# Differential heads' probabilities and two heads' rows turned by VectorE and transfers, in a decoder layer on one Trainium2 core

## The chip, the cores and the metric

One core of one Trainium2 chip runs the whole layer in one launch. The metric is the device time in microseconds, the median of three runs. All times below are microseconds unless marked ns.

The engines are called as in the profile: PE is TensorE, ACT is ScalarE, DVE is VectorE, POOL is GpSimd (used here to issue transfers), SP is SyncE (which issues the weight loads).

## The reference

A decoder layer in float32: half a SwiGLU feed-forward, a token mixer with two attention branches, another half feed-forward, with layer norms between. One batch, 256 positions, 2048 channels, 5632 hidden. The change lies in the mixer:

```python
def _diff_attention(q, k, v, positions, lam):
    ...
        s = jnp.einsum('bqhmd,bkhmd->bhmqk', q[:, q0:q1], k[:, :q1]).astype(jnp.float32) * scale
        dist = jnp.abs(pos[:, q0:q1, None] - pos[:, None, :q1])
        s = s - slopes[None, :, None, None, None] * dist[:, None, None, :, :]
        s = jnp.where(_causal_mask(q0, q1), s, -jnp.inf)
        p = jax.nn.softmax(s, axis=-1)
        a = (p[:, :, 0] - lam * p[:, :, 1]).astype(v.dtype)
        outs.append(jnp.einsum('bhqk,bkhd->bqhd', a, v[:, :q1]))

def _mixer(...):
    ...
    o_mla = _mla_attention(q, k, v_mla).reshape(b, s, MLA_V_COLS)
    o_diff = _diff_attention(...)
    o_diff = (_rms_norm(o_diff, subln_g) * (1.0 - lambda_init)).reshape(b, s, DIFF_V_COLS)
    y = jax.nn.sigmoid(gate_mla) * (o_mla @ w_br_mla) + jax.nn.sigmoid(gate_diff) * (o_diff @ w_br_diff)
    return y @ w_out
```

There are 4 differential heads, each with two maps of 128 channels and values of 256, and 8 MLA heads with values of 128.

## The kernel before

**Matmuls.** The 256 rows lie in two blocks (b = 0, 1) of 128. A large product is made in three matmuls (`triple`, L208 to L210) from a high and a low part of each operand, so that it keeps float32's precision. SP streams the weights into `raw` tiles of 512 KB (two k-tiles of 128x512). ACT casts each to its high part (`wring`, L154), DVE subtracts it from the raw tile for the low part (`wring`, L155), into a ring of 6 pairs in the mixer. One raw tile serves one **unit**, 12 matmuls (2 k-tiles x 3 x 2 blocks). A cast waits until PE has used the ring's pair.

**Order.** The program is written as a chain of units. `later(n, fn)` has `fn` issued n units further on; this is how the small work (softmax, turns, copies) is put between the units. The numbers in the `later` calls are thus a table of due times, and a scheduler sets the final order on each engine from what the program issues. Each engine then runs its own list in order.

**Mixer.** In order of units: a latent projection; the gates (rows kept in DRAM by `keep_gate`, L1197 and L1199); dq, dk (`pair_cols`, L1210) and dv; wuq, wuk and wuv for MLA; the last gate chunks; `branch_diff` for four quads f of 512 output channels (x = od, the differential heads' outputs); `branch_mla` for the same four (x = om). After that w_out takes y. The work of the differential heads (`diff_head`) is spread over the wuq, wuk and wuv units and the gates'.

**A differential head** has four steps: `scores` (8 matmuls, L1250, and two softmaxes; the difference p at L1259), `turn`, `values` (three pairs of matmuls, L1270 to L1272, then an RMS norm, `junk` on ACT and `orow` on DVE), `turn2` (orow turned and cast into `od`). p is 128 x 384: the block pairs (0,0), (1,0), (1,1).

**Turning.** What enters a matmul must have its channels, or keys, on the partitions. There are two ways to turn a 128x128 piece. One is a transpose on PE with the identity into a PSUM bank, followed by a copy (`p_cols` L1108, `turn2` L1290, `rows_to_quad` L671). The other is `turn` (L722): DVE transposes in blocks of 32x32 (`blocks`, L715), four transfers on POOL's queue write the rows to DRAM so that the blocks land in order (`turn`, L717), and `wait` units later one transfer reads it back (`turned`, L729); `more` units later it is used. Its channels lie in an order of their own, and the rows of the weight are put into the same order on the host (`_turned_rows`). `turn_p` (L1116) does this for the p of the MLA heads with one transfer out (`pturn`) and four back (`pt`).

**The gates back.** `get_gates(f)` (L1350) has POOL load the four gate tiles of quad f (two branches, two blocks, 256 KB each, L1354). `branch_mla(f)` makes the sigmoids on ACT (L1371), multiplies the diff branch by its gate (L1374), and when a block's product is done, L1375 and L1376 add the MLA branch. y of f = 0 and 1 is turned by transfers, y of f = 2 and 3 by PE (`rows_to_quad`, L671).

**POOL's queue** issues its transfers in list order, over 8 semaphores in turn: the ninth transfer after one waits for it to have landed.

Of the kernel before, what the change touches and what calls it, by code (L numbers as in the profile page):

```python
# [11 lines left out]
F32 = mybir.dt.float32  # L12
# [47 lines left out]
def layer_kernel(ctx: ExitStack, tc: tile.TileContext, a: dict, out: bass.AP):  # L60
# [27 lines left out]
    def tr_bank(name="tr"):  # L88
        return psum.tile([P, 512], F32, tag="tr", name=nm(name), bufs=3)
# [633 lines left out]
    def turn(row, use, wait, more):  # L723
        to = dram.tile([P, 512], F32, name=nm("turn"))
        turn_out(row, to)

        def back():
            t = tmp_tile([P, 512], "turned")
            nc.gpsimd.dma_start(t, to)  # L729
            later(more, lambda: use(turned(t)))  # L730
        later(wait, back)

    def turn_to_quad(row, b, x, q, wait, more):
        turn(row, lambda t: x.put(q, b, t), wait, more)

    def turn_to_cols(row, dst, b, wait, more):
        turn(row, lambda t: S.copy(dst[:, :, b * P:(b + 1) * P].rearrange("p k (i c) -> p k i c", i=4), t), wait, more)
# [367 lines left out]

    SEG = ((0, P), (P, 384))

    def p_cols(p):  # L1108
        t = tr_bank()
        for i in range(3):  # L1110
            PE.transpose(t[:, i * P:(i + 1) * P], p[:, i * P:(i + 1) * P], ident)
        pt = small.tile([P, 384], F32, tag="p", name=nm("pt"), bufs=3)
        S.copy(pt, t[:, 0:384])
        return pt

    def turn_p(p, keep, more):  # L1116

        t = tmp_tile([P, 384], "pblocks")
# [12 lines left out]
    def mixer(x):  # L1131
# [76 lines left out]
        def pair_cols(w, name):  # L1208
            dst = [act_tile([P, 4, T], F32, name) for _ in range(2)]

            def done(n, b, bank, snap, op):
                t = tmp_tile([P, 512], name + "r")
                whole(t, bank, snap, op)
                later(1, lambda: turn_to_cols(t, dst[n], b, 4, 10))
            hy.group(w[0], w[1], done, False, True)
            return dst

# [19 lines left out]
            project((a["wgm"], a["wgd"])[i][f], x, KD, 512, lambda b, bank: keep_gate(i, f, b, bank))  # L1237

        od = Acts(MH, "od")

        def diff_head(h):
            st = {}
# [18 lines left out]
                st["p"] = p1  # L1261

            def turn():
                st["pt"] = p_cols(st["p"])

            def values():
                pt = st["pt"]
                o = tr_bank()
                dvh = [t[:, h * DV:(h + 1) * DV] for t in dv]
                PE.matmul(o[:, 0:DV], pt[:, 0:P], dvh[0], start=True, stop=True)  # L1270
                PE.matmul(o[:, DV:2 * DV], pt[:, P:T], dvh[0], start=True, stop=False)
                PE.matmul(o[:, DV:2 * DV], pt[:, T:384], dvh[1], start=False, stop=True)  # L1272
                ss = sm(2, "oss")
                junk = tmp_tile([P, 512], "junk")
                for b in range(2):
                    S.activation(junk[:, b * DV:(b + 1) * DV], o[:, b * DV:(b + 1) * DV], AF.Square,
                                 accum_out=ss[:, b:b + 1])
                ms = sm(2, "oms")
                V.tensor_scalar(out=ms, in0=ss, scalar1=1.0 / DV, scalar2=None, op0=ALU.mult)
                r = rstd(ms, RMS_EPS, 2)  # L1280
                orow = tmp_tile([P, 512], "orow")
                for b in range(2):
                    V.scalar_tensor_tensor(out=orow[:, b * DV:(b + 1) * DV], in0=o[:, b * DV:(b + 1) * DV],
                                           scalar=r[:, b:b + 1], in1=subg, op0=ALU.mult, op1=ALU.mult)
                st["o"] = orow

            def turn2():
                t = tr_bank()
                for i in range(4):
                    PE.transpose(t[:, i * P:(i + 1) * P], st["o"][:, i * P:(i + 1) * P], ident)  # L1290
                tv = t.rearrange("p (b i t) -> p b i t", b=2, i=2)
                for b in range(2):
                    od.put(h // 2, b, tv[:, b], (h % 2) * 2, 2)
            return scores, turn, values, turn2

        for h in range(DH):
            for i, f in enumerate(diff_head(h)):
                later(2 + 5 * h + 3 * i + i // 3, f)
        qT = [cols_proj(a["wuq"][c], cn, 4, "qT") for c in range(2)]
        qrT = act_tile([P, 4, T], F32, "qrT")  # L1300

# [65 lines left out]
        def branch_mla(f):  # L1367
            g0, g1 = gates.pop(f)
            y = diff_rows.pop(f)
            for t in (g0, g1):  # L1370
                S.activation(t, t, AF.Sigmoid)  # L1371

            def done(b, bank):
                V.tensor_tensor(out=y[:, b, :], in0=y[:, b, :], in1=g1[:, b, :], op=ALU.mult)  # L1374
                V.tensor_tensor(out=g0[:, b, :], in0=bank, in1=g0[:, b, :], op=ALU.mult)  # L1375
                V.tensor_tensor(out=y[:, b, :], in0=y[:, b, :], in1=g0[:, b, :], op=ALU.add)  # L1376
                if f < 2:
                    later(1, lambda: turn_to_quad(y[:, b, :], b, yq, f, 4, 6))
                else:
                    later(2, lambda: rows_to_quad(y[:, b, :], b, yq, f))  # L1380
            project(a["wbm"][f], om, MH, 512, done)
# [74 lines left out]
def _layout(i):  # L1456
# [25 lines left out]
    r["wuk"] = _chunks(_turned_rows(_turned_cols(w["mla_w_uk"])), 512)  # L1482
    r["wuv"] = _chunks(_turned_rows(w["mla_w_uv"]), 512)
    r["wbm"] = _chunks(w["w_branch_mla"], 512)
    r["wbd"] = _chunks(w["w_branch_diff"], 512)
    r["w_out"] = _chunks(np.concatenate([_turned_rows(w["w_out"][:1024]), w["w_out"][1024:]]), 512)
    pos = i["positions"]
    r["pos_row"] = pos.reshape(1, T)
# [31 lines left out]
```

## Time and profile before

| | us |
|---|---|
| median of three runs | 1967.29 (1966.77 to 1968.22) |
| the profiled execution | 1969.03 |
| its span on the chip | 1967.3 |
| PE busy in it | 1951.7 (99%) |
| DVE busy | 1777.8 (90%) |
| ACT busy | 1249.7 (64%) |
| POOL busy | 309.3 (16%) |
| granted TensorE clock | 0.998 |

The span is the time from the first to the last instruction; the rest of the execution's time lies around it. A row of the timeline gives start, duration, engine, line, operation, out<-in, tile and how many of the same kind; in brackets, how long the engine was idle before, and what ended it. Matmuls overlap, so a row's duration is longer than its distance to the next. The stage of the differential heads runs from about 987 to 1074, the MLA heads from 1075 to 1143, `branch_mla` from 1143 to 1188.

### The profile page before, as it was taken

To read this page: it belongs to the slowest core of one execution; us is meant where nothing else is said; L and a number is where in the kernel's file an instruction comes from. 1 tells how busy PE (TensorE), PEld (TensorE's weight loads), DVE (VectorE), ACT (ScalarE), POOL (GpSimd) and SP (SyncE) were. 2 spreads that over 40 slices of the span, in tenths; PEclk is the share of its full clock that TensorE was granted. 3 is DMA by queue.
4 is the path that set the end of the run, shared out by engine and by line. 5 is a ranking of instruction groups with operands and counts; after the bars stand their busy time and mean duration, and the time that the engine had idled before them with its cause. 6 is when DMAs were issued, how large, how long until landed. Compare 5 with 4: busy or idle time off the path is not lost.

```text
span 1967.3 us, 25772 instructions
## 1 busy us (share of the span) xinstructions
PE 1951.7 (99%) x8760; PEld 1618.2 (82%) x8760; DVE 1777.8 (90%) x2183; ACT 1249.7 (64%) x1634; POOL 309.3 (16%) x531
## 2 busy tenths in 40 slices
PE   9999999999999999999999999999999999999997
PEld 8888888888888898888888887888888888888886
DVE  7999999998998879988987676789999999999986
ACT  6666766676655666666667654556676666765661
POOL 0112111122100010102241530001211112210000
PEclk9999999999999999999999999999999999999999
DMA  8978888878776666767685788678888878787773
GB/s 315 285 227 262 268 261 247 259 234 306 271 238 214 208 223 248 246 223 262 203 248 196 236 295 274 198 261 255 255 267 264 250 238 271 251 314 236 277 233 121
DMA packets 149779, 488.83 MB, mean 248 GB/s; under 512 B 21600, under 2 KB 21648, under 8 KB 149648
## 3 DMA queue, kind: packets, MB, share of 16 engines
q1 hardware_dynamic: 119088, 401.13, 59.5%
q0 software_dynamic: 30560, 86.07, 16.8%
q8 instruction: 68, 1.11, 0.2%
q14 instruction: 63, 0.52, 0.1%
HBM read 456.71 MB, written 30.41 MB: 248 GB/s over the span
## 4 chain that ended last, share of the span: by engine, by line
PE 92%; DMA 3%; DVE 1%; issue 1%; ACT 1%; POOL 1%; SPq 0%; DVEq 0%; POOLq 0%; ACTq 0%
PE mm L209 29%; PE mm L208 29%; PE mm L210 29%; DMA turned<-turn 1%; DMA gate<-gates 1%; PE tr L210 1%; PE tr L209 1%; PE tr L208 1%; DMA turn<-blocks 0%; POOL turn L717 0%; PE tr L671 0%; ACT wring L154 0%; DMA raw<-in_wgd_dram 0%; DMA raw<-in_gu_dram 0%; PE tr L1322 0%
## 5 line engine op out<-in xcount | busy, mean ns | idle before, releaser
L154 ACT CAST wring<-raw 128x1024 fp32r<-128x1024 f32 (+2 forms) x467 | 481.9, 1037 | 322.3 <-PE mm L210 236.7
L155 DVE TENSOR_TENSOR wring<-raw,wring 128x1024 fp32r<-128x1024 f32 (+2 forms) x467 | 557.4, 1201 | 91.7 <-ACT wring L154 89.4
L154 ACT CAST wring<-sraw 128x1024 fp32r<-128x1024 f32 x436 | 453.0, 1052 | 201.9 <-DVE sraw L428 85.7
L155 DVE TENSOR_TENSOR wring<-sraw,wring 128x1024 fp32r<-128x1024 f32 x436 | 520.7, 1219 | 23.6 <-ACT wring L154 20.7
L208 PE MATMUL mm<-wring,h 128*128 128x512 f32 (+2 forms) x1248 | 480.9, 385 | 0.0
L210 PE MATMUL mm<-wring,h 128*128 128x512 f32 (+2 forms) x1248 | 480.3, 385 | 0.0
L209 PE MATMUL mm<-wring,h 128*128 128x512 f32 (+2 forms) x1248 | 480.0, 385 | 0.0
L208 PE MATMUL mm<-wring,xs 128*128 128x512 f32 x776 | 302.2, 389 | 0.6 <-ACT snap L385 0.6
L209 PE MATMUL mm<-wring,xs 128*128 128x512 f32 x776 | 301.9, 389 | 0.0
L210 PE MATMUL mm<-wring,xs 128*128 128x512 f32 x776 | 301.9, 389 | 0.0
L208 PEld LDWEIGHTS mm<-wring,h 128*128 128x128 f32 x1248 | 234.5, 188 | 46.9 <-ACT h L154 0.6
L209 PEld LDWEIGHTS mm<-wring,h 128*128 128x128 f32 x1248 | 234.5, 188 | 46.5 <-DVE wring L155 0.4
L210 PEld LDWEIGHTS mm<-wring,h 128*128 128x128 f32 x1248 | 234.4, 188 | 46.5 <-DVE h L155 0.7
L428 DVE TENSOR_TENSOR sraw<-sraw,sraw 128x1024 f32<-128x1024 f32 x168 | 199.2, 1219 | 2.0 <-DMA sraw<-in_wgm_dram 1.2
L208 PEld LDWEIGHTS mm<-wring,xs 128*128 128x128 f32 x776 | 145.7, 188 | 31.2 <-ACT snap L385 1.0
L210 PEld LDWEIGHTS mm<-wring,xs 128*128 128x128 f32 x776 | 145.7, 188 | 30.2
L209 PEld LDWEIGHTS mm<-wring,xs 128*128 128x128 f32 x776 | 145.7, 188 | 30.1
L717 POOL DMA_DIRECT2D hT<-blocks x176 | 96.8, 562 | 367.0 <-DVE blocks L715 366.0
L209 PE MATMUL mm<-wring,x 128*128 128x512 f32 x336 | 130.8, 389 | 0.5 <-DVE wring L155 0.5
L208 PE MATMUL mm<-wring,x 128*128 128x512 f32 x336 | 130.8, 390 | 0.0
L210 PE MATMUL mm<-wring,x 128*128 128x512 f32 x336 | 130.6, 389 | 0.0
L430 POOL DMA_DIRECT2D sraw<-in_gu_dram x40 | 35.5, 889 | 371.3 <-DVE sraw L428 288.3
(310 smaller groups left out, 2286.7 us busy)
## 6 DMA issues: line engine op xcount, KB each, us to landing
sraw<-in_gu_dram SPq DMA_DIRECT2D x160, 512.0 KB, 5.2
raw<-in_gu_dram SPq DMA_DIRECT2D x159, 512.0 KB, 4.9
raw<-in_dn_dram SPq DMA_DIRECT2D x140, 512.0 KB, 4.7
sraw<-in_gu_dram POOLq DMA_DIRECT2D x40, 512.0 KB, 7.1
sraw<-in_dn_dram SPq DMA_DIRECT2D x36, 512.0 KB, 5.2
eraw<-in_gu_dram SPq DMA_DIRECT2D x64, 256.0 KB, 5.8
raw<-in_w_out_dram SPq DMA_DIRECT2D x32, 512.0 KB, 4.3
hraw<-hT POOLq DMA_DIRECT2D x56, 256.0 KB, 5.8
```

The lines of the kernel that those rows point to most:

```text
L154: cast[0] = S.copy(hi, src)
L155: lows[0] = V.tensor_tensor(out=lo, in0=src, in1=hi.bitcast(F32), op=ALU.subtract)
L208: PE.matmul(o, xh, wh, start=first, stop=False, skip_group_check=again)
L209: PE.matmul(o, xh, wl, start=False, stop=False, skip_group_check=again)
L210: PE.matmul(o, xl, wh, start=False, stop=last, skip_group_check=again)
L428: last = V.tensor_tensor(out=R[src][i], in0=R[src][i], in1=R[add[1]][i], op=ALU.add)
L430: nc.gpsimd.dma_start(R["12"][s], source("22", s), accum_op=ALU.add)
L717: nc.gpsimd.dma_start(to.rearrange("(g r) (i f) -> i r g f", g=4, i=4)[i], t[32 * i:32 * (i + 1), :].rearrange("r (g f) -> r g f", g=4))
```

## The change

p of the differential heads is turned by `turn_p`, as with the MLA heads, and `p_cols` goes. The four steps' due times within a head go from 0, 3, 7, 10 to 0, 3, 9, 11. The output rows of heads 0 and 1 go into one tile, `orows`, and a new function `turn_both` turns both blocks with one DVE transpose of 128x1024, four transfers out and one back; the first 512 rows of the diff branch's weight are put in the matching order on the host. Heads 2 and 3 keep their transposes on PE. y of f = 0 and 1 uses `turn_both` too, once its second block is done, in place of one `turn` for each block. The copies of the turned dq and dk are due 8 units after the load back instead of 10.

```diff
--- before.py
+++ after.py
@@ -730,8 +730,21 @@
             later(more, lambda: use(turned(t)))
         later(wait, back)
 
-    def turn_to_quad(row, b, x, q, wait, more):
-        turn(row, lambda t: x.put(q, b, t), wait, more)
+    def turn_both(rows, use, wait, more):
+
+        t = act_tile([P, 2, 512], F32, "blocks")
+        V.transpose(t.rearrange("p b f -> p (b f)"), rows.rearrange("p b f -> p (b f)"))
+        to = dram.tile([P, 2, 512], F32, name=nm("turn"))
+        for i in range(4):
+            nc.gpsimd.dma_start(to.rearrange("(g r) b (i f) -> i r b g f", g=4, i=4)[i],
+                                t[32 * i:32 * (i + 1)].rearrange("r b (g f) -> r b g f", g=4))
+
+        def back():
+            t = act_tile([P, 2, 512], F32, "turned")
+            nc.gpsimd.dma_start(t, to)
+            for b in range(2):
+                later(more + b, lambda b=b: use(b, turned(t[:, b, :])))
+        later(wait, back)
 
     def turn_to_cols(row, dst, b, wait, more):
         turn(row, lambda t: S.copy(dst[:, :, b * P:(b + 1) * P].rearrange("p k (i c) -> p k i c", i=4), t), wait, more)
@@ -1105,14 +1118,6 @@
 
     SEG = ((0, P), (P, 384))
 
-    def p_cols(p):
-        t = tr_bank()
-        for i in range(3):
-            PE.transpose(t[:, i * P:(i + 1) * P], p[:, i * P:(i + 1) * P], ident)
-        pt = small.tile([P, 384], F32, tag="p", name=nm("pt"), bufs=3)
-        S.copy(pt, t[:, 0:384])
-        return pt
-
     def turn_p(p, keep, more):
 
         t = tmp_tile([P, 384], "pblocks")
@@ -1211,7 +1216,7 @@
             def done(n, b, bank, snap, op):
                 t = tmp_tile([P, 512], name + "r")
                 whole(t, bank, snap, op)
-                later(1, lambda: turn_to_cols(t, dst[n], b, 4, 10))
+                later(1, lambda: turn_to_cols(t, dst[n], b, 4, 8))
             hy.group(w[0], w[1], done, False, True)
             return dst
 
@@ -1237,6 +1242,7 @@
             project((a["wgm"], a["wgd"])[i][f], x, KD, 512, lambda b, bank: keep_gate(i, f, b, bank))
 
         od = Acts(MH, "od")
+        orows = act_tile([P, 2, 512], F32, "orow")
 
         def diff_head(h):
             st = {}
@@ -1261,7 +1267,7 @@
                 st["p"] = p1
 
             def turn():
-                st["pt"] = p_cols(st["p"])
+                turn_p(st["p"], st, 2)
 
             def values():
                 pt = st["pt"]
@@ -1278,13 +1284,21 @@
                 ms = sm(2, "oms")
                 V.tensor_scalar(out=ms, in0=ss, scalar1=1.0 / DV, scalar2=None, op0=ALU.mult)
                 r = rstd(ms, RMS_EPS, 2)
-                orow = tmp_tile([P, 512], "orow")
+                if h < 2:
+                    orow = [orows[:, b, h * DV:(h + 1) * DV] for b in range(2)]
+                else:
+                    st["o"] = tmp_tile([P, 512], "orow")
+                    orow = [st["o"][:, b * DV:(b + 1) * DV] for b in range(2)]
                 for b in range(2):
-                    V.scalar_tensor_tensor(out=orow[:, b * DV:(b + 1) * DV], in0=o[:, b * DV:(b + 1) * DV],
+                    V.scalar_tensor_tensor(out=orow[b], in0=o[:, b * DV:(b + 1) * DV],
                                            scalar=r[:, b:b + 1], in1=subg, op0=ALU.mult, op1=ALU.mult)
-                st["o"] = orow
 
             def turn2():
+                if h == 0:
+                    return
+                if h == 1:
+                    turn_both(orows, lambda b, t: od.put(0, b, t), 2, 4)
+                    return
                 t = tr_bank()
                 for i in range(4):
                     PE.transpose(t[:, i * P:(i + 1) * P], st["o"][:, i * P:(i + 1) * P], ident)
@@ -1295,7 +1309,7 @@
 
         for h in range(DH):
             for i, f in enumerate(diff_head(h)):
-                later(2 + 5 * h + 3 * i + i // 3, f)
+                later(2 + 5 * h + (0, 3, 9, 11)[i], f)
         qT = [cols_proj(a["wuq"][c], cn, 4, "qT") for c in range(2)]
         qrT = act_tile([P, 4, T], F32, "qrT")
 
@@ -1375,7 +1389,8 @@
                 V.tensor_tensor(out=g0[:, b, :], in0=bank, in1=g0[:, b, :], op=ALU.mult)
                 V.tensor_tensor(out=y[:, b, :], in0=y[:, b, :], in1=g0[:, b, :], op=ALU.add)
                 if f < 2:
-                    later(1, lambda: turn_to_quad(y[:, b, :], b, yq, f, 4, 6))
+                    if b == 1:
+                        later(1, lambda: turn_both(y, lambda n, t: yq.put(f, n, t), 2, 5))
                 else:
                     later(2, lambda: rows_to_quad(y[:, b, :], b, yq, f))
             project(a["wbm"][f], om, MH, 512, done)
@@ -1482,7 +1497,7 @@
     r["wuk"] = _chunks(_turned_rows(_turned_cols(w["mla_w_uk"])), 512)
     r["wuv"] = _chunks(_turned_rows(w["mla_w_uv"]), 512)
     r["wbm"] = _chunks(w["w_branch_mla"], 512)
-    r["wbd"] = _chunks(w["w_branch_diff"], 512)
+    r["wbd"] = _chunks(np.concatenate([_turned_rows(w["w_branch_diff"][:512]), w["w_branch_diff"][512:]]), 512)
     r["w_out"] = _chunks(np.concatenate([_turned_rows(w["w_out"][:1024]), w["w_out"][1024:]]), 512)
     pos = i["positions"]
     r["pos_row"] = pos.reshape(1, T)
```

How the instructions move: on **ACT**, while the wuv units run (kTr is the copy of a wuk product's bank, v that of a wuv product's, od the output rows turned by PE). Before:

```order
L1183 COPY kTr_8109<-mm_8075 128x512
L154 CAST od_8192<-tr_8183 128x256
L154 CAST wring_114<-raw_8415 128x1024
L737 COPY qT_7824<-turned_8061 128x4x128
L1311 COPY v_8135<-mm_8176 128x512
L737 COPY qT_7824<-turned_8090 128x4x128
L1311 COPY v_8134<-mm_8241 128x512
L1183 COPY kTr_8153<-mm_8111 128x512
L154 CAST wring_104<-raw_8459 128x1024
```

and now:

```order
L1188 COPY kTr_8065<-mm_8031 128x512
L154 CAST wring_116<-raw_8341 128x1024
L1188 COPY kTr_8086<-mm_8052 128x512
L154 CAST wring_114<-raw_8401 128x1024
L154 CAST wring_104<-raw_8425 128x1024
L154 CAST wring_102<-raw_8442 128x1024
L1188 COPY kTr_8128<-mm_8088 128x512
L1282 ACTIVATE junk_8135,oss_8134<-tr_8130 128x256 x2
L692 ACT_TABLE_LOAD
```

The fourth kTr copy stood behind copies of v and qT, ahead of the cast into wring_104; it now stands behind the casts into wring_114, wring_104 and wring_102. The casts of od for heads 0 and 1 are gone from here, and the work of head 1's output (junk, sd) has come behind it.

On **POOL**, as `branch_mla` begins (gate_9368 to gate_9463 before are the gates of f = 2 and 3; turn and turned are y's). Before:

```order
L1126 DMA pt_9208<-pturn_9155 32x12x32 x4
L1354 DMA gate_9368<-gates 128x512 x2
L1354 DMA gate_9369<-gates 128x512 x2
L1354 DMA gate_9462<-gates 128x512 x2
L1354 DMA gate_9463<-gates 128x512 x2
L717 DMA turn_9374<-blocks_9375 32x4x128 x4
L717 DMA turn_9403<-blocks_9404 32x4x128 x4
L729 DMA turned_9468<-turn_9374 128x512
L729 DMA turned_9499<-turn_9403 128x512
L717 DMA turn_9470<-blocks_9471 32x4x128 x4
L717 DMA turn_9501<-blocks_9502 32x4x128 x4
```

and now:

```order
L1131 DMA pt_9214<-pturn_9161 32x12x32 x4
L760 DMA cols_9654<-in_ln_cols_dram 128x32
L1368 DMA gate_9374<-gates 128x512 x2
L1368 DMA gate_9375<-gates 128x512 x2
L739 DMA turn_9404<-blocks_9402 64x4x128 x4
L744 DMA turned_9442<-turn_9404 128x1024
L1368 DMA gate_9463<-gates 128x512 x2
L1368 DMA gate_9464<-gates 128x512 x2
L739 DMA turn_9493<-blocks_9491 64x4x128 x4
L744 DMA turned_9531<-turn_9493 128x1024
```

The gates of f = 3 (gate_9462 and gate_9463 before, gate_9463 and gate_9464 now) stood ahead of y's first turn. They now stand behind the load back of y's quad 0 (turned_9442), which waits for its four transfers out.

On **DVE**, in the same stage (wring of L155 is the low part of a weight tile; diff_8963 and diff_8969 are the rows of f = 1, diff_9110 and diff_9116 those of f = 2, diff_9219 those of f = 3). Before:

```order
L715 STREAM_TRANSPOSE blocks_9502<-diff_8963 128x512
L155 TENSOR_TENSOR wring_105<-raw_9625,wring_104 128x1024
L155 TENSOR_TENSOR wring_103<-raw_9645,wring_102 128x1024
L1375 TENSOR_TENSOR gate_9368<-mm_9483,gate_9368 128x512
L1376 TENSOR_TENSOR diff_9110<-diff_9110,gate_9368 128x512
L155 TENSOR_TENSOR wring_5086<-raw_9668,wring_5085 128x1024
L1375 TENSOR_TENSOR gate_9368<-mm_9518,gate_9368 128x512
L1376 TENSOR_TENSOR diff_9110<-diff_9110,gate_9368 128x512
L155 TENSOR_TENSOR wring_119<-raw_9697,wring_118 128x1024
```

and now:

```order
L736 STREAM_TRANSPOSE blocks_9491<-diff_8969 128x1024
L155 TENSOR_TENSOR wring_103<-raw_9633,wring_102 128x1024
L1389 TENSOR_TENSOR gate_9374<-mm_9475,gate_9374 128x512
L1390 TENSOR_TENSOR diff_9116<-diff_9116,gate_9374 128x512
L1388 TENSOR_TENSOR diff_9219<-diff_9219,gate_9464 128x512 x2
L155 TENSOR_TENSOR wring_5086<-raw_9658,wring_5085 128x1024
L1389 TENSOR_TENSOR gate_9374<-mm_9508,gate_9374 128x512
L155 TENSOR_TENSOR wring_119<-raw_9689,wring_118 128x1024
L1390 TENSOR_TENSOR diff_9116<-diff_9116,gate_9374 128x512
L155 TENSOR_TENSOR wring_117<-raw_9717,wring_116 128x1024
```

The product of f = 3's diff rows with their gate (L1388) used to come far ahead, behind that of f = 2. It now stands between the sum for block 0 and the sum for block 1 of f = 2, which PE's second L671 transposes take as input.

## The prediction

> **What bounds the kernel now.** I read the page first: the busy times and the chain.
>
> ```profile
> PE 1951.7 (99%) x8760; PEld 1618.2 (82%) x8760; DVE 1777.8 (90%) x2183; ACT 1249.7 (64%) x1634; POOL 309.3 (16%) x531
> PE 92%; DMA 3%; DVE 1%; issue 1%; ACT 1%; POOL 1%; SPq 0%; DVEq 0%; POOLq 0%; ACTq 0%
> ```
>
> TensorE is busy all the time, so the time is the number of its instructions times their pitch, plus its few gaps. Next I read its waits (line waited at, releaser, us in total, times, longest), and the groups of the transposes that go.
>
> ```profile
> PE tr L671 <- DVE diff L1376: 1.8, 1, 1.8
> PE tr L1111 <- DVE p L1259: 0.3, 1, 0.3
> L1290 PE MATMUL tr<-ident,orow 128*128 128x128 f32 x16 | 2.9, 274 | 0.0
> L1111 PE MATMUL tr<-ident,p 128*128 128x128 f32 x12 | 2.7, 282 | 0.3 <-DVE p L1259 0.3
> ```
>
> All that can be won is therefore small: 20 of these 28 transposes (all 12 of p, 8 of 16 of orow), and two waits that lie in the functions of the diff. What can be lost isn't in this list: waits that TensorE doesn't have yet.
>
> **Gains on TensorE.** The durations of the groups overlap with other matmuls, so I take the price from the timeline: how far matmuls stand apart with and without a transpose among them.
>
> ```profile
> 997.62 0.40 PE L208 MATMUL mm<-wring,cn 128*128 128x512 f32 x1
> 997.86 0.27 PE L1111 MATMUL tr<-ident,p 128*128 128x128 f32 x1
> ...
> 998.43 0.38 PE L1111 MATMUL tr<-ident,p 128*128 128x128 f32 x2
> 998.57 0.47 PE L208 MATMUL mm<-wring,cn 128*128 128x512 f32 x1
> 998.88 0.39 PE L209 MATMUL mm<-wring,cn 128*128 128x512 f32 x1
> 1072.42 0.40 PE L210 MATMUL mm<-wring,h 128*128 128x512 f32 x1
> 1072.65 0.60 PE L1290 MATMUL tr<-ident,orow 128*128 128x128 f32 x4
> 1073.01 0.48 PE L208 MATMUL mm<-wring,h 128*128 128x512 f32 x1
> 1073.32 0.39 PE L209 MATMUL mm<-wring,h 128*128 128x512 f32 x1
> 1041.61 0.39 PE L210 MATMUL mm<-wring,h 128*128 128x512 f32 x1
> 1042.32 0.30 PE L1111 MATMUL tr<-ident,p 128*128 128x128 f32 x1 [0.32 <-DVE p L1259]
> 1185.25 0.39 PE L210 MATMUL mm<-wring,om 128*128 128x512 f32 x1
> 1187.49 0.63 PE L671 MATMUL tr<-ident,diff 128*128 128x128 f32 x4 [1.84 <-DVE diff L1376]
> ```
>
> Weight matmuls follow each other at 0.227 (1072.42 to 1072.65). From 997.62 to 998.88 there are four of them (two in the "..."), 4 x 0.227 = 0.91, and the three transposes of p cost the rest of 1.26: 0.35. Four heads: 1.4. From 1072.42 to 1073.32 there are two, 0.45, and the four of orow cost 0.45. Two heads: 0.9. The wait before p of head 2 is 1042.32 - 1041.61 - 0.23 = 0.48 and goes with the transposes. **Gains: 1.4 + 0.9 + 0.48 = 2.8.** The last two rows are the other wait, 2.24 - 0.23 = 2.0, ahead of the transposes of y's quad f = 3, block 0; it is treated below.
>
> [...]
>
> **New waits in the attention.** p now goes through DVE, one transfer out and four back. The MLA heads do this already, so its price has rows.
>
> ```profile
> 1041.82 0.74 DVE L1259 SCALAR_TENSOR_TENSOR p<-p,rs,p 128x128 f32<-128x128 f32 x2
> 1050.40 0.59 PE L1270 MATMUL tr<-dv,pt 128*128 128x256 f32 x2
> L1119 DVE STREAM_TRANSPOSE pblocks<-p x8: 567/578/580, 1075.2 to 1122.5; 128x384 f32<-128x384 f32 x8
> 1076.11 0.54 POOL L1121 DMA_DIRECT2D pturn<-pblocks  x1 [10.37 <-DVE pblocks L1119]
> 1078.53 1.99 POOL L1126 DMA_DIRECT2D pt<-pturn  x3 [1.89 <-DMA pturn<-pblocks]
> 1082.76 0.64 POOL L1126 DMA_DIRECT2D pt<-pturn  x1 [1.10 <-issue]
> DMA to landing us min/median/max: 3.0/4.9/8.0
> L1338 PE MATMUL tr<-pt,v x16: 377/377/378, 1089.4 to 1137.8; 128*128 128x256 f32 x16
> ```
>
> From p to pt: 1.2 for a weight subtraction that may stand ahead on DVE, 0.6 pblocks, 0.3 to the issue, 2.4 from that to the first pt (1076.11 to 1078.53), 2.0 to the fourth, 4.9 to its landing: 11.4 us, or 9.5 to 14.5 with the ends of the landing. In return the values move back. Counted in TensorE's two orders, the weight matmuls between a head's scores and its values are 72, 75, 104, 55 before and 117, 154, 131, 102 now. Heads 0 and 1 get 10 and 18 us more by that, enough. Head 3 gets 47 x 0.227 = 10.7, enough too. Head 2 gets least, 27 x 0.227 = 6.1 us: p is ready at 1042.56, the values at 1050.40 move, against the scores, by 6.1 less the 0.48 + 0.35 + 0.45 that go between them, to 1055.2; p + 11.4 is 1054.0. The margin is 1.2 at the median landing, and -1.9 at the longest; I take 0.9 of waiting, halfway. MLA's head 0: its last pt was issued at 1082.76 and landed by the median at 1087.7, for values at 1089.4. Its scores now come 12 matmuls later (2.7 us), its values 2 later (0.5), so 1090.4 stands against 1089.9: 0.4 after what the gains take off. One more comes from ACT:
>
> ```profile
> 1027.55 0.59 ACT L1183 COPY kTr<-mm 128x512 f32<-128x512 f32 x1
> 1028.44 1.05 ACT L154 CAST wring<-raw 128x1024 fp32r<-128x1024 f32 x1 [0.30 <-PE mm L210]
> ```
>
> A cast waits until TensorE has used a ring pair. The copy that frees the bank for the first matmul of the diff gate now stands right behind such a cast (first piece of the order above), and TensorE reaches that bank about 6 matmuls, 1.4 us, after it freed the pair: cast 1.05 + copy 0.59 + some 0.2 for each of the two hand-overs is 2.1, so 0.7 late. Below nothing it can't go; above, one whole unit, 2.7. **Attention: 0.9 + 0.4 + 0.7 = 2.0, between 0 and 6.** orow of heads 0 and 1 goes through one transfer far ahead of its use (the first od product comes after all MLA scores); it costs POOL five issues, covered by POOL's 16%. The copies of dq and dk "2 units sooner" move no row of any engine; nothing.
>
> **The y stage.** Here the order on POOL changes most (second piece above): the four gate loads of f = 3 stood ahead of y's first turn, and now stand behind the load that waits for that turn to land.
>
> ```profile
> 1131.43 0.57 POOL L1354 DMA_DIRECT2D gate<-gates  x1 [1.27 <-DMA gate<-gates]
> 1136.14 2.12 POOL L1354 DMA_DIRECT2D gate<-gates  x4 [0.80 <-issue]
> 1157.72 2.17 POOL L717 DMA_DIRECT2D turn<-blocks  x4 [0.87 <-DVE blocks L715]
> 1137.72 10.01 DMA gate<-gates
> 1147.76 1.07 ACT gate L1371
> 1159.35 5.02 DMA turn<-blocks
> 1176.64 6.99 DMA turned<-turn
> 1186.65 0.70 DVE diff L1376
> 1176.85 0.60 PE L671 MATMUL tr<-ident,diff 128*128 128x128 f32 x4
> L154 ACT CAST wring<-raw 128x1024 fp32r<-128x1024 f32 (+2 forms) x467 | 481.9, 1037 | 322.3 <-PE mm L210 236.7
> L155 DVE TENSOR_TENSOR wring<-raw,wring 128x1024 fp32r<-128x1024 f32 (+2 forms) x467 | 557.4, 1201 | 91.7 <-ACT wring L154 89.4
> ```
>
> Both blocks of y's quad 0 are transposed together about a microsecond sooner than the second block was, so the turns leave at some 1156.5 to 1159 and land 5.0 later, at 1163 to 1164. Only then does POOL issue the load back, then the four gate loads at 1163.9 to 1166.1. A gate load took up to 10.0 with eight of them under way; here it has 512 KB of y and three gates ahead of it, so I take 8.5 from the last issue at 1165.6: the last gate lands at L = 1174, with 1171.9 and 1176.1 as bounds (6.3 and 10.5).
>
> Who waits: DVE multiplies these gates into diff of f = 3 ahead of the sums of f = 2's second block (third piece above), whose transposes TensorE reaches at 1176.85. After L: sigmoid 1.06, two products 1.3, weight subtraction 1.2, gate 0.7, weight subtraction 1.2, diff 0.7 = 6.2. So the gate decides once L is above 1176.85 - 6.2 = 1170.65, and TensorE waits L - 1170.65 = **3.3**, between 1.3 and 5.4. In exchange the old 2.0 goes: the load back of y's quad 1 (issued about 1176, landed by 1183.6 as before) is followed by only y, gate and diff, 2 us, ready at 1186, and TensorE with 3.3 us more behind it is there at 1188.
>
> [...]
>
> **Sum.** -2.8 - 2.0 + 2.0 + 3.3 = +0.5. The profiled execution took 1969.03 (span 1967.3), 1.7 above the median of 1967.29; a difference made in the one holds for the other: **1967.8**. About 0.2%, 3.9 us, is what a measurement of this kernel can tell from no change.
>
> **Rivals.**
> *The new waits don't arise (0.20).* pt lands ahead of its use and the gates land by 1170.7. For it: the median landing of pt leaves head 2 a margin of 1.2. Against it: the gate load's 10.01. Then -2.8 - 2.0, with up to 1 us left of the wait at 1187: -4.3, 1963.0.
> *A transpose is worth its duration (0.05).* TensorE would lose 5.5 in place of 2.3: 0.5 - 3.2 = -2.7, 1964.6. Against it stand the rows at 0.11. [...]
> *The gates of f = 3 land late (0.15), slower.* The place is POOL's queue at the y turn, the price one microsecond of TensorE for each that L is above 1170.65. The eight loads from 1131.43 to 1147.73 moved 2.1 MB in 16.3 us, 129 GB/s; at 100 GB/s, three quarters of that, the 1.57 MB of y and gates from 1163.5 on end at 1179, a wait of 8.3: +5.5, 1972.8. From L = 1177.4 on it makes the kernel slower by more than the 3.9 us told of above.
> *The values come late (0.12), slower.* POOL's queue takes more than the 11.4, or the landing is 8.0, in more than one head: two heads late by 3 us in place of 0.9: +5, 1972.5. Then the trace has TensorE waiting at tr<-dv,pt.
>
> **How the numbers follow.** Forecast 0.48: gains and new waits cancel, by its own bounds from -3.5 (all low ends) to +4.5; 1967.8. Faster is the first rival: 0.20. Slower are the two late ones: 0.27. The rest, 0.53, is the same. The range reaches to the first rival on the one side and into the late cases on the other, where they begin to be unlikely: 1962.8 to 1973.0.
>
> **What would show it.** In the trace after: no L1111 rows and 8 transposes of orow; TensorE waiting in the f = 2 quad's second transpose for DVE's diff, with the last gate load of f = 3 landing at 1172 to 1176; no wait or a shorter one at the f = 3 quad; short waits for pt at head 2, MLA's head 0, and for a kTr copy. The prediction is wrong if the gates land ahead of 1170 or behind 1178, if a wait at tr<-dv,pt is above 2 us, or if a wait shows up that none of these places has, on the wring above all (POOL and SP share the transfers).

## The result and the profile after

The change makes the kernel slower: 1978.49 us (median of 4 runs, 1974.48 to 1979.36) against 1967.03 for the kernel before (4 runs, 1966.12 to 1968.22). The ratio is 1.0054, with a 95% interval of 1.0036 to 1.0071: 7 to 14 us. The forecast was 1967.8, its range 1962.8 to 1973.0.

The first rows of the page and TensorE's waits of the changed kernel, from its profiled execution of 1974.48 (line waited at, releaser, us in total, times, longest), and the group of transposes that is left:

```profile
PE 1949.7 (99%) x8740; PEld 1615.0 (82%) x8740; DVE 1779.1 (90%) x2184; ACT 1249.9 (63%) x1630; POOL 320.7 (16%) x546
PE tr L1276 <- DMA pt<-pturn: 3.2, 2, 2.5
PE tr L671 <- DVE diff L1390: 3.0, 2, 2.2
PE mm L208 <- ACT kTr L1188: 2.4, 1, 2.4
L1304 PE MATMUL tr<-ident,orow 128*128 128x128 f32 x8 | 1.6, 275 | 0.0
```

The 20 transposes are gone (8760 to 8740 matmuls), and three waits head the list: two that it did not have, and the one at L671, which now comes twice, at f = 2 and f = 3, in place of once at f = 3. They are at the places that the prediction named: values of head 2 and 3 for pt, the bank that the fourth kTr copy frees, and the transposes of y behind the late gates. In TensorE's timeline each shows as the distance between two matmuls, less the 0.23 of one:

```profile
1026.54 0.39 PE L210 MATMUL mm<-wring,cn 128*128 128x512 f32 x1
1029.31 0.50 PE L208 MATMUL mm<-wring,h 128*128 128x512 f32 x1 [2.38 <-ACT kTr L1188]
...
1054.76 0.39 PE L209 MATMUL mm<-wring,h 128*128 128x512 f32 x1
1057.61 0.67 PE L1276 MATMUL tr<-dv,pt 128*128 128x256 f32 x2 [2.47 <-DMA pt<-pturn]
...
1180.49 0.39 PE L210 MATMUL mm<-wring,om 128*128 128x512 f32 x1
1183.09 0.63 PE L671 MATMUL tr<-ident,diff 128*128 128x128 f32 x4 [2.21 <-DVE diff L1390]
```

They cost 2.54, 2.62 and 2.37. With 0.84 at head 3's values, 0.65 at an MLA head and 0.92 at y's f = 3 the new waits come to 9.94. That is nearly the whole of this execution: from 1966.78, a profiled execution of the kernel before that has neither of the two old waits (before_2 below, the fastest of its ten), less 2.3 for the transposes, plus 9.94, is 1974.4. From 1968.01, another without them (before_3), it would be 1975.7, so the sum is good to about 1 us.

But this was the fastest of the four runs. The others took 1978 to 1979 at a mean granted clock of 0.995 to 0.996, where this one has 0.998. What lies in these 4 us was the first thing to find out.

### The profile page after: what moved, and what is told of

Read it like the earlier page. It is cut to its first block, busy times and chain, and to the rows that moved or that the text cites. A ratio compares the mean times of both kernels' runs of the same rounds, so it can differ in the third digit from the quotient of the medians.

```text
span 1972.6 us, 25757 instructions
## 1 busy us (share of the span) xinstructions
PE 1949.7 (99%) x8740; PEld 1615.0 (82%) x8740; DVE 1779.1 (90%) x2184; ACT 1249.9 (63%) x1630; POOL 320.7 (16%) x546
## 5 line engine op out<-in xcount | busy, mean ns | idle before, releaser
L155 DVE TENSOR_TENSOR wring<-raw,wring 128x1024 fp32r<-128x1024 f32 (+2 forms) x467 | 556.4, 1200 | 94.0 <-ACT wring L154 91.9
L155 DVE TENSOR_TENSOR wring<-sraw,wring 128x1024 fp32r<-128x1024 f32 x436 | 520.2, 1217 | 22.1 <-ACT wring L154 19.1
```

Of the source, the lines that this page charges most:

```text
L155: lows[0] = V.tensor_tensor(out=lo, in0=src, in1=hi.bitcast(F32), op=ALU.subtract)
```

## The experiments

The table gives each run's median beside the kernel before on the same chips. Expectations are quoted as they stood before the runs.

| run | what it is | us | ratio to before (95%) |
|---|---|---|---|
| again | the change | 1978.27 | 1.0051 (1.0039 to 1.0064) |
| p_back | the change, p on PE | 1973.23 | 1.0025 (1.0013 to 1.0036) |
| y_back | the change, y's blocks apart | 1976.16 | 1.0040 (1.0026 to 1.0053) |
| o_back | the change, all orow on PE | 1975.73 | 1.0042 (1.0030 to 1.0055) |
| pb_own | the change, pblocks in p's buffers | 1978.20 | 1.0046 (1.0034 to 1.0058) |
| g28 | the change, gates of f = 2 and 3 earlier | 1980.61 | 1.0061 (1.0047 to 1.0075) |
| c2 | pblocks as in pb_own, gates of f = 3 earlier, head 2's values later | 1974.18 | 1.0037 (1.0024 to 1.0050) |
| y_g28 | before, joint y and earlier gates | 1972.17 | 1.0020 (1.0012 to 1.0029) |
| y_alone | before, joint y | 1971.85 | 1.0023 (1.0013 to 1.0033) |
| p_alone | before, p by transfers | 1971.59 | 1.0018 (1.0009 to 1.0027) |
| o_alone | before, orow of heads 0, 1 by transfers | 1970.94 | 1.0012 (1.0003 to 1.0021) |
| q1pe | before, y's quad 1 on PE | 1969.41 | 1.0007 (0.9998 to 1.0015) |
| before_2 | before | 1967.59 | 1.0000 (0.9991 to 1.0010) |

before_3, the kernel before once more, had a single execution, of 1968.01, and no interval.

### again: the change once more

No edit.

> The changed kernel once more. Its profiled execution took 1974.5 at a mean granted clock of 0.998, its three timed ones 1978 to 1979 at 0.995 to 0.996. Theory (clock): behind one of the new waits of 2.5 us the granted clock falls for some microseconds in most executions, which costs some 4 us on top of the waits; then the executions fall into two groups, near 1974.5 at 0.998 and near 1978.5 at 0.995, and a profile of the second group shows a dip of the clock right behind a wait of 2.5 us or more. Rival (landing): the timed executions just wait longer for the transfers; then time and clock do not go together.

Measured: 1980.02, 1978.27, 1977.12, 1979.54 and 1975.19 us at clocks of 0.995, 0.996, 0.996, 0.995 and 0.997. Time and clock go together. The profile is that of the execution of 1980.02; here is TensorE around the kTr bank, and then the windows of the trace (stretch in us, its length, busy time of PE, PEld, DVE, ACT and POOL, the granted clock, DMA share and GB/s):

```profile
1027.46 0.39 PE L210 MATMUL mm<-wring,cn 128*128 128x512 f32 x1
1032.08 0.80 PE L208 MATMUL mm<-wring,h 128*128 128x512 f32 x1 [4.23 <-ACT kTr L1188]
1032.67 0.63 PE L209 MATMUL mm<-wring,h 128*128 128x512 f32 x1
1033.10 0.63 PE L210 MATMUL mm<-wring,h 128*128 128x512 f32 x1
```

```profile
1031.90:1037.50 5.60, 5.42 (x13) 4.26 (x14) 3.45 (x13) 5.57 (x14) 3.54 (x7) 0.50 0.75 235
1183.00:1188.00 5.00, 0.72 (x4) 0.26 (x2) 4.82 (x7) 4.60 (x7) 0.56 (x1) 1.00 0.64 235
1188.00:1191.50 3.50, 3.41 (x10) 2.90 (x11) 2.88 (x4) 0.00 (x0) 0.00 (x0) 0.51 0.99 364
```

The waits are longer here, 4.39 at the bank and 4.52 at y, and behind each the clock is halved: matmuls follow each other at 0.43 (1032.67 to 1033.10) in place of 0.23. The two dips, of 6.8 and 3.4 us, hold 10.2 us at half the clock; in 1.1 of them TensorE still waited, so they cost half of the rest, 4.6. Both readings hold a part: the slower execution has single waits that are longer, and the dips. But all its waits together are 10.6, against 9.9 in the first profile, so most of the difference is the dips. 1966.78 less 2.3, plus 10.6 and 4.6, is 1979.7; measured was 1980.02. Between 980 and 1220 of the 16 profiles every dip has a granted clock of 0.50 and lasts 3.4 us or 6.8; not every long wait has one (last section).

Why the bank came so late stands in ACT's row of this execution:

```profile
1031.44 0.59 ACT L1188 COPY kTr<-mm 128x512 f32<-128x512 f32 x1 [2.51 <-DMA pturn<-pblocks]
```

The copy waits for a transfer that has nothing to do with kTr. Its target is one of the six small buffers that all the temporary tiles share, and the one whose turn it is still holds pblocks, the transposed p of a differential head, until that has been written to DRAM. In the first profile the copy waited 0.66 more behind the same buffers (for DVE's transpose of an earlier tile).

### p_back, y_back, o_back: one part undone

p_back:

```diff
-                turn_p(st["p"], st, 2)
+                st["pt"] = p_cols(st["p"])
...
-                later(2 + 5 * h + (0, 3, 9, 11)[i], f)
+                later(2 + 5 * h + 3 * i + i // 3, f)
```

> The change without the turn of p by transfers (p turned on PE, old due times). The trace of the changed kernel has 2.5 us of waiting for the kTr copy, 2.6 and 0.8 for pt and 0.6 in the MLA heads, 6.6 in all, for which 1.4 + 0.5 come back. Theory (waits of the attention, then the clock): the profile loses 4.7 us against the changed kernel's 1974.5, to 1969.8, and with the waits of 2.5 us gone there also go the dips of the clock: the median is near 1970. Rival (the y stage drops the clock): the waits go, the clock stays at 0.995, median 1974. Rival (transfers as such): the 30 more transfers slow the rest, and most of the loss stays.

Measured: 1973.23, 5.0 below the change, so of the three parts undone p is the largest; but not the 1970 that was expected. It is nearer to the first rival's 1974, though the clock, 0.996 to 0.998, did not stay at 0.995. The waits for pt and for the kTr bank are gone. Two others have grown: 3.16 at y's f = 2, with a dip of 3.4 us behind it, and 2.23 at head 2's transposes of p, in place of the 0.48 in the first profile of the kernel before. That wait's rows, on DVE and on PE:

```profile
1041.92 0.17 DVE L1116 RECIPROCAL rs<-sums 128x2 f32<-128x2 f32 x1 [2.09 <-ACT p L1114]
1043.34 0.30 PE L1124 MATMUL tr<-ident,p 128*128 128x128 f32 x1 [2.08 <-DVE p L1273]
```

DVE waits 2.1 for ACT's exponentials, and TensorE for p.

y_back:

```diff
-                    if b == 1:
-                        later(1, lambda: turn_both(y, lambda n, t: yq.put(f, n, t), 2, 5))
+                    later(1, lambda: turn_to_quad(y[:, b, :], b, yq, f, 4, 6))
```

> The change without the joint turn of y (each block turned on its own as before). The waits of 2.4 and 0.9 at the transposes of f = 2 and 3 go, the old wait of 2.0 comes back: 1.3 less in the profile. Theory (waits of the attention, then the clock): 1973.2 for an execution without a dip, median near 1977. Rival (the y stage drops the clock): median near 1973.

Measured: 1976.16, as the first theory had it; the waits of the attention, 4.6 at the bank and 2.2 at pt, keep their dips, so it isn't the y stage alone that drops the clock. In its profiled execution, its slowest (1981.37), there are three dips, of 6.8, 3.4 and 3.4 us, which cost 6.2.

o_back:

```diff
-                if h < 2:
-                    orow = [orows[:, b, h * DV:(h + 1) * DV] for b in range(2)]
...
-                if h == 0:
-                    return
-                if h == 1:
-                    turn_both(orows, lambda b, t: od.put(0, b, t), 2, 4)
-                    return
```

> The change with the rows of heads 0 and 1 turned on PE as before. Costs 0.9 of transposes. Theory (order on ACT): the fourth kTr copy now stands behind one gated cast fewer, so of the 2.5 us of waiting for it some or all goes: 1972.5 to 1975.5 without a dip. Rival (the outputs' transfers delay head 3's or MLA's pt): the waits for pt of 0.8 and more go as well, -1 more.

Measured: 1975.73, 2.5 less, though it does 8 transposes more. The kTr wait is gone, as the theory said: the copy no longer stands behind the third gated cast, and the buffer it takes is another. The waits for pt did not go: 2.9 and 1.1. The profile is that of its slowest execution (1979.49); it also has 4.6 at y's f = 2, and dips of 3.4 and 6.8 us.

### pb_own, g28, c2: three repairs

pb_own gives the differential heads' pblocks a buffer of p's own:

```diff
-        t = tmp_tile([P, 384], "pblocks")
+        t = (small.tile([P, 384], F32, tag="p", name=nm("pblocks"), bufs=3) if own
+             else tmp_tile([P, 384], "pblocks"))
...
-                turn_p(st["p"], st, 2)
+                turn_p(st["p"], st, 2, True)
```

> The change, but the blocks of p (pblocks) of the differential heads take a buffer of p's own three, not one of the six shared small buffers. ACT's order up to the fourth kTr copy stays as in the change. Theory (shared buffer): that copy waits for the transfer that empties pblocks (2.5 us in the profile of the second execution of the change, where TensorE waited 4.2); now it follows its cast at once, TensorE waits 2.0 to 2.5 there at most, and no dip of the clock follows it. The median comes 3 to 5 us below the change's 1978.3: 1973 to 1975. Rival (gated cast): the copy is late because it stands behind a cast that waits for TensorE; then the wait stays at 2.5 to 4.2 and the median at 1977 to 1978.

ACT's rows, and TensorE's:

```profile
1027.75 1.04 ACT L154 CAST wring<-raw 128x1024 fp32r<-128x1024 f32 x1 [0.30 <-PE mm L210]
1028.82 0.58 ACT L1189 COPY kTr<-mm 128x512 f32<-128x512 f32 x1
```

```profile
1027.32 0.39 PE L210 MATMUL mm<-wring,cn 128*128 128x512 f32 x1
1029.45 0.50 PE L208 MATMUL mm<-wring,h 128*128 128x512 f32 x1 [1.74 <-ACT kTr L1189]
```

The mechanism is as the theory had it: the copy follows its cast at once, and the wait at the bank is 1.9 in place of 2.5 and 4.4. These 1.9 are the gated cast, the copy and their hand-overs: TensorE stops at the very matmul that the cast waits for (it ends at 1027.71, the cast starts at 1027.75), not 6 matmuls later. In the profiles in which the blocks share a buffer and the copy stands behind the same three casts, the bank's wait is 2.5, 4.4, 4.6 (y_back) and 4.0 (g28); with the own buffer it is 1.9 and, in c2, 1.8. The median did not follow: 1978.20, which is the rival's time, though the rows are the theory's. Executions lie at 1973.9 and 1974.2, and at 1978.2 to 1979.8; the profile is the one of 1973.9, without a dip, with 2.6 at head 2's pt and 2.8 at y left. What the slower ones wait for, no profile shows, and their clocks of 0.996 and 0.997 do not tell dips from longer waits.

g28:

```diff
-        for f, at in enumerate((16, 20, 28, 32)):
+        for f, at in enumerate((16, 20, 26, 28)):
```

> The change, with the gates of f = 3 due at 28 instead of 32, which puts their loads ahead of y's first turn on POOL's queue. Theory (gates behind the turn): the wait at the second transposes of f = 2 (2.4 in the first profile, 4.4 in the second) goes, some 1 to 2 us remain at f = 3, where the load back of y's quad 1 lands late as in the kernel before; with the dip behind the longer wait gone too the median falls by 3 to 5 us: 1973.5 to 1975.5. Rival (y's turn itself is late): the wait moves from f = 2 to f = 3 and the time stays at 1977 to 1978.

The edit does more than the expectation says: the gates of f = 2 are due at 26 instead of 28 as well. The rival held in the place of the wait. With the gates ahead of the turn nothing is waited for at f = 2, but at f = 3 it is 2.76. (c2 and y_g28 below leave the gates of f = 2 at 28 and wait at f = 3 too, so the 26 is not the reason.) On POOL, ACT and PE:

```profile
1172.97 2.43 POOL L739 DMA_DIRECT2D turn<-blocks  x4 [0.71 <-DVE blocks L736]
1182.34 0.56 POOL L744 DMA_DIRECT2D turned<-turn  x1 [6.94 <-DMA turn<-blocks]
```

```profile
1189.46 1.14 ACT L154 CAST y<-turned 128x512 fp32r<-128x512 f32 x2 [4.86 <-DMA turned<-turn]
```

```profile
1194.28 0.63 PE L671 MATMUL tr<-ident,diff 128*128 128x128 f32 x4 [2.60 <-DVE diff L1390]
```

The joint turn of quad 1 can't start before its second block is done, and all of its 512 KB go out (from 1172.97 to 1182.3) before the load back begins, which lands at 1189.5. DVE's diff for f = 3 stands behind y's casts, and TensorE behind it. The median is 1980.61, not better than the change and above the rival's 1977 to 1978; the 4.0 at the kTr bank was still there in the profile, with a dip of 6.8 us.

c2 has the own buffer, the gates of f = 3 due at 28 (those of f = 2 stay at 28), and this:

```diff
-                later(2 + 5 * h + (0, 3, 9, 11)[i], f)
+                later(2 + 5 * h + (0, 3, 9 + 2 * (h == 2), 11 + 2 * (h == 2))[i], f)
```

> Both of these, and the values and output of head 2 due two units later (132 weight matmuls from its scores to its values in place of 125 with the own buffer alone). Theory: all new waits above 2.5 us are gone, and with them the dips; what is left of them is some 2 at the kTr bank, 1 at f = 3 and 1 to 2 at head 2's pt. Gains 2.8 + 2.0 against new waits of 4 to 5: 1967 to 1970, the same as before. Rival (transfers as such slow the stage): 1973 or more.

```profile
PE tr L671 <- DVE diff L1391: 3.3, 1, 3.3
PE mm L208 <- ACT kTr L1189: 1.6, 1, 1.6
PE tr L1277 <- DMA pt<-pturn: 1.3, 2, 1.0
```

Measured: 1974.18, 4.1 below the change but far from the 1967 to 1970 expected. The attention's waits fell from 6.6 to about 3; y's wait, at f = 3, is 3.43, with a dip of 3.4 us behind it, which costs 1.4. The time is the rival's, but the rows show these waits and no general slowing: 1966.78 less 2.3, plus 3.0, 3.4 and 1.4, is 1972.3, and the profiled execution took 1973.01.

### The parts alone, in the kernel before

> The kernel before with only the joint turn of y and the gates of f = 3 due at 28. Theory (the old wait came from the load back of y's quad 1 behind quad 0's, on one queue): with half as many transfers, and none of the gates between, the 2.0 at f = 3 falls to 0 to 1, and nothing is added: 1966.5 to 1968.5 against 1968.5 for the kernel before on this chip, or 1 us less in the mean. Rival (the joint turn waits for its second block, so quad 1 lands later): the wait at f = 3 grows to 3 or more and the time to 1970 or more.

Measured: 1972.17 (the edits are the joint turn and the gates' due times 16, 20, 28, 28). The rival held in the time, 4 us slower; the wait at f = 3, 2.1, is smaller than its 3, in a profile of 1969.96, one of the quicker executions (1968.9 to 1975.0). The load back of quad 1 leaves at 1177.7 and lands at 1183.5 there; in before_2 the second block's leaves at 1174.3 and lands at 1180.1.

> The kernel before with only the joint turn of y. Theory: the gates of f = 3 stand behind y's turn again, so TensorE waits some 2.5 to 4.5 at the second transposes of f = 2, and 0 to 1 at f = 3, in place of 2.0 there; above 3 us a dip of the clock follows. 1970 to 1973 against 1968. Rival (the joint turn costs nothing by itself, its loss in the change comes from the attention's delay): 1967 to 1968.5.

Measured: 1971.85. Its profile of 1971.0 waits 2.06 at f = 2 and 1.22 at f = 3: the forecast's places, the first a little below its 2.5 to 4.5, the second a little above its 0 to 1. This is without the attention's delay and without a dip.

> The kernel before with only p turned by transfers (and its due times). Gains 1.9 (transposes, old wait). Theory: TensorE waits for pt at heads 2 and 3 as in the change without the joint rows (2.9 and 1.1 there), with a dip behind the longer wait in some executions; the y stage is as before: 1970 to 1973. Rival (the three parts only hurt together): 1966 to 1968.

Measured: 1971.59. The profile waits 2.2 and 0.9 at the values of heads 2 and 3, with a dip of 3.4 us behind the first, and nothing at f = 3.

> The kernel before with only the rows of heads 0 and 1 turned by transfers. Gains 0.9. Theory: PE's order shifts head 2's scores so that p comes later against its transposes, as in the change without the turn of p (2.2 of waiting there in place of 0.5): 1968 to 1970. Rival (that wait came from the joint turn's other parts): 1967, 0.9 below the kernel before.

Measured: 1970.94. TensorE waits 2.41 for p at head 2, with a dip of 3.4 us. The edit is not on that path: it moves the scheduler's order on TensorE (the scores of head 2 come 6 matmuls sooner, its p is wanted 79 matmuls behind them instead of 78). TensorE is there 1.9 sooner than in before_2 (1040.2 against 1042.1), and p comes 0.9 later. The three parts alone add 4.1, 3.8 and 3.2 to the 1967.79 of the kernel before, 11.0 in all; the change as a whole adds 9.7 (again) to 11.5. The parts add up in the sum only. The wait at the kTr bank, 2.5 to 4.4 in the change, is in none of the three profiles of the parts, and o_alone's wait for p ahead of its transposes can't be in the change, where these transposes are gone. That the sums meet is not shown to be more than chance. The sooner copies of dq and dk were not run alone; up to the first turn of p, long behind them, every engine's order is the same before and after.

### q1pe: without the last transfers of y

```diff
-                if f < 2:
+                if f < 1:
                     later(1, lambda: turn_to_quad(y[:, b, :], b, yq, f, 4, 6))
```

(with the rows of w_out in the order that goes with it)

> The kernel before with only y's quad 0 turned by transfers, quads 1 to 3 by PE. Costs 8 transposes at 0.11, 0.9; the 16 transposes' worth of queue ahead of the last load back go, and with it the wait of 2.0 at f = 3. Theory: 1.1 less than before, 1966.8 against 1968. Rival (DVE waits for quad 0's second load back ahead of f = 2, which lands at 1170.7): TensorE waits up to 3 at f = 2 instead, 1969 to 1972.

Measured: 1969.41. This is in the rival's range of time, but by neither's mechanism. TensorE waits nowhere in the y stage, so DVE did not get in the way; but there was no gain either, and the 8 transposes alone are 0.9 of the 1.6. The interval of the ratio holds 1. It looked as if the wait of 2.0 at f = 3 was not there to be won.

### before_2 and before_3: the kernel before, two more profiles

> The kernel before itself, for a second profile. Theory: the wait of 2.0 at f = 3, on which 2.0 of the forecast's gains rest, isn't in its typical execution (the profiled one took 1969.0, 1.2 more than the median of 30): here 0 to 1 at f = 3, some 0.5 at head 2's p, no dip, near 1967.5. Rival: the wait of 2.0 is always there, and the 1.2 are scatter of something else. Against itself the ratio must hold 1 in its interval.

> The kernel before once more, for a third profile. By the theory the wait at f = 3 is 0 to 1 again and the time near 1967.5; by the rival the wait is 2.0 and the time 1968 to 1969.

TensorE of before_2 (1966.78) at the two old waits, then ACT at the load back of y's quad 1:

```profile
1041.87 0.39 PE L210 MATMUL mm<-wring,h 128*128 128x512 f32 x1
1042.11 0.27 PE L1111 MATMUL tr<-ident,p 128*128 128x128 f32 x1
...
1184.99 0.40 PE L210 MATMUL mm<-wring,om 128*128 128x512 f32 x1
1185.22 0.60 PE L671 MATMUL tr<-ident,diff 128*128 128x128 f32 x4
```

```profile
1180.14 0.62 ACT L154 CAST y<-turned 128x512 fp32r<-128x512 f32 x1 [1.30 <-DMA turned<-turn]
```

Neither wait is there: 0.24 and 0.23 between the rows, one matmul each. The load of y's quad 1 landed at 1180.1; in the first profile, at 1183.7. before_3 (1968.01) has neither of them as well. So 2.5 of the 4.8 us that the forecast counted as gains were in one of three profiled executions. They are about the 2.2 us between the profiled 1969.03 and before_2; before_3 shows that executions without them still differ by 1.2.

## Why the prediction was wrong, step by step

From the forecast of 1967.8 to the 1978.49 measured it is 10.7 us. By the steps below 2.5 of them are gains that were not there, 4.6 the attention's waits, none the y stage's in the first profile, and some 4 what the other executions take above that profile, the dips of the clock above all; these come to 11.

**The gains: 2.3 instead of 4.8.** The price of a transpose, 0.11 in a stream of matmuls, fits: with it the two sums above come within 0.4 of the profiled executions from before_2, and within 1.2 from before_3; at 0.274 each, the mean duration of orow's group in the kernel before, on which the rival's 5.5 for 20 rests, the first would have been 1971.2 or 1972.5, for 1974.48. The two waits counted beside it, 0.48 and 2.0, were the failure. "A difference made in the one holds for the other" took the waits of one profiled execution for those of the median, though the text had noted that this execution stood 1.7 above it.

**Attention: forecast 2.0, between 0 and 6; measured 6.6 in the first profile.** The mechanisms and the places were right, three sizes were not.

The kTr bank was forecast at 0.7 and cost 2.5 and 4.4. The "about 6 matmuls" of room ahead of the bank were none, which makes 1.9 (pb_own), and the copy's target buffer was left out altogether. It is a resource of which the change takes a new share: p's blocks hold a shared buffer from their transpose until their transfer has landed, and the copy waited 2.51 for that in again.

Head 2's pt was forecast at 0.9 and cost 2.6. The path in the changed kernel, on DVE and on POOL:

```profile
1043.81 0.74 DVE L1265 SCALAR_TENSOR_TENSOR p<-p,rs,p 128x128 f32<-128x128 f32 x2
```

```profile
1046.47 0.55 POOL L1126 DMA_DIRECT2D pturn<-pblocks  x1 [5.79 <-DVE pblocks L1124]
1051.70 2.67 POOL L1131 DMA_DIRECT2D pt<-pturn  x4 [4.68 <-DMA pturn<-pblocks]
```

From the issue of pturn to the first pt it took 5.2; the one row that the forecast had used says 2.4. From p (1044.55) to the values (1057.61) it became 13.1 instead of 11.4, and TensorE got there 10.4 after p was ready (1054.76 and one matmul), not 12.6. Head 3, forecast to have room enough, cost 0.8. MLA's head 0, forecast at 0.4, cost nothing; head 1 cost 0.65. The prediction's own sign of being wrong, a wait at tr<-dv,pt above 2 us, was there.

**The y stage: forecast 3.3, with the old wait of 2.0 gone; measured 2.4 at f = 2 and 0.9 at f = 3 in the first profile, 4.5 at f = 2 in the second.** This step was right in place and mechanism, and within its bounds of 1.3 to 5.4 in size. POOL and ACT of the first profile:

```profile
1160.04 2.46 POOL L739 DMA_DIRECT2D turn<-blocks  x4 [19.91 <-DVE blocks L736]
1167.23 0.56 POOL L744 DMA_DIRECT2D turned<-turn  x1 [4.74 <-DMA raw<-in_wbm_dram]
1167.78 2.14 POOL L1368 DMA_DIRECT2D gate<-gates  x4
```

```profile
1177.08 1.06 ACT L1385 ACTIVATE gate<-gate 128x1024 f32<-128x1024 f32 x1 [1.41 <-DMA gate<-gates]
```

The stage began 3.9 later than in the kernel before. The gates left at 1167.8, behind the turn (forecast 1163.9, with the delay the same), the last was there at 1177.1, and TensorE went on 6.0 later (forecast 6.2). What was missed is that earlier gates would not have helped: quad 1's joint turn is late by itself (g28, c2, y_g28).

**What no step had: the clock.** The sum took a wait for what it lasts. In the 16 profiles, between 975 and 1200, there are 8 gaps of 3.15 us or more from one matmul to the next, and with each the granted clock falls to a half; of the 16 from 2.0 to 3.1, it falls with four. A dip of 3.4 us costs 1.4 to 1.7 us, one of 6.8 costs 2.8 to 3.0: half of its length, less what lies in the wait. The dips, and the longer single waits with which they come, put the median some 4 us above the first profiled execution. Why this one has no dip at all, with gaps of 2.77, 2.85 and 2.60, no run shows (last section).

**The chances.** Slower had 0.27, split over two rivals, late gates and late values. Values came late at two heads, but at 2.6 and 0.8 us, not 3 each; the gates were late by the main forecast's own size, not by the rival's 8.3. So slower came true by other terms than the rivals': the kTr bank, the clock and the missing gains. The range was also too narrow by its own bounds: with attention at 6 and y at 5.4 the sum is -2.8 - 2.0 + 6 + 5.4 = +6.6, 1973.9, not the +4.5 that it gives as its upper end.

Open is what the slower executions of pb_own wait for, and why ACT's exponentials come later in o_alone and p_back; their order changes, but no run separates which instruction does it.

## What to carry to other kernels

When a compute engine is busy 99% of the time, a transfer put in the place of a transpose wins only the transpose's pitch (0.11 us here), while a landing that comes late costs the wait (2.62 at head 2's pt) and perhaps a dip of the clock: 12 of the 24 gaps of 2.0 us or more had one here, at 1.4 to 3.0 us each. Before work is moved to transfers, list what buffers its tiles hold until the transfer lands and who takes these buffers next; and count a wait as won only if it is in more than one profile of the kernel. Joining two blocks in one transfer saves issues, but makes the first block wait for the second.

## What the runs showed of the hardware

The length of a gap between two matmuls did not tell by itself whether the clock falls. At one of 2.28 us the granted clock went to 0.50 for 3.4 us (y_back, at 1196), and another of 3.07 passed at 1.00 (pb_own, at 1180.5). Between 975 and 1200 of the 16 profiles, all 8 gaps of 3.15 to 4.86 us came with a dip; of the 16 from 2.01 to 3.07 us the four that did were 2.28 and 2.45 (y_back), 2.43 (p_alone) and 2.64 (o_alone). The 2.24 of the kernel before and the 2.77, 2.85 and 2.60 in the first profile of the change had none. What sets the two kinds apart was not shown: no run was made to test it.

Landing times differ by microseconds from one execution to the next (y's load back at 1180.1 and at 1183.7 in the kernel before): the kernel before takes most of that up in its slack (the later of the two cost it the wait of 2.0) and spreads over 3.3 us in 30 runs (1966.58 to 1969.92), g28 over 9.6 in 6 (1974.94 to 1984.57).
